# Slots and distances of the weight blocks, two steps of head 0 and the v statistics of a two-layer hybrid kernel

## The chip, the cores and the metric

One core of one Trainium2 chip runs the whole program. Its engines work beside each other, each on its own list of instructions: TensorE multiplies (PE in the profile, PEld for its weight loads), VectorE (DVE) and ScalarE (ACT) work elementwise, SyncE (SP) and GpSimd (POOL) issue transfers here. They wait for each other by semaphores. The metric is device time in microseconds (us), the median of several runs.

## The reference

Two layers over 512 latent tokens of 1024 features and 256 context tokens: layer 0 mixes the tokens by bidirectional retention with 4 heads, layer 1 by a gated unit with a spatial product (gMLP). All arithmetic is in float32.

```
for i in range(DEPTH):                       # DEPTH = 2
    shift, scale, gate = split(silu(c) @ ada_w[i] + ada_b[i])
    hx = rmsnorm(x, norm_g[i]) * (1 + scale) + shift      # hc alike, from the context
    if i == 0:   out = retention_mixer(hx, hc, ...)        # q, k, v, z = hx @ w_in; scores * decay; @ w_out
    else:        out = gmlp_chunk_mixer(hx, ...)
    x = x + gate * out
return rmsnorm(x, final_g)

def gmlp_chunk_mixer(h, w_in, vnorm_g, w_s, b_s, w_out):
    u, v, z = h @ w_in[:, :W], h @ w_in[:, W:2*W], h @ w_in[:, 2*W:]
    v = v - mean(v);  v = v * rsqrt(mean(v * v) + eps) * vnorm_g
    mixed = einsum('gij,bnjgc->bnigc', w_s, v in chunks of 128) + b_s
    return (u * mixed * silu(z)) @ w_out
```

## The kernel before

**How a product is made.** TensorE multiplies float32 in a short form, so each operand is split in two: ScalarE casts it to that form (the high half, a CAST), VectorE subtracts the high half from the operand (the low half, a TENSOR_TENSOR), and `mm3` sums three products: low x high, high x low, high x high. Weight matrices are cut in 2 x 2 blocks, and of each such product only seven are taken instead of eight (names B11, B21, T1, T2, B22, T3, T4). The T products need a difference of two weight blocks first; VectorE takes it in place, the first raw block minus the second (`raw<-raw`). The operand on the other side is a sum or difference too (the tiles `oA..`, `oS1` to `oS4`, and `rows` for the 256 context tokens).

**How weights come.** A `Stream` Q holds the order of all products and their loads. A load takes the first free slot of its list (`W` in line 215: w0 to w6, at times g0), SyncE transfers the raw block there, `upto` makes the difference and the split two products ahead of the one that TensorE is at, and `drop` frees the slot. The halves go to one of four rooms of 2112 columns with the tag hl; `split_tile` (line 97) puts them at an offset that `FORMS` (line 88) names for each kind of product: kq, v, z for layer 0's projections, wo for its output, v1 for layer 1's v, u for its u and z blocks, o for its output. All tiles stand in the order of the list in lines 91 to 95, so the list sets the addresses: slot w4 stands ahead of the 8 columns of gate0, the other w slots behind them. `t2` tiles, eleven of 512 columns, serve for what is short-lived, such as a score (pf) and its halves (ph, pl).

**What sets the order.** Every engine works off its list in the order of the text (class Queue, which records each operation, so that all of them show as line 55; transfers show as line 129). Where something is not due at once, it stands in a generator, and `aside` takes one step of it at a chosen product.

**The stages the text below speaks of:**
- V01 is the v projection of heads 0 and 1. Beside it `sums` lets VectorE and ScalarE make the operands: `sum_s2`, `sum_s4`, `sum_s3` work on the blocks of the normed input (f11, f12, f21, f22, each 1024 columns of a tile xq, in slots s0 to s3), `rows_s1` to `rows_s4` on the context (cq). `rows_s2` (line 798) writes `rows` into slot s1, f12's.
- Z23 is the z projection of heads 2 and 3, the last one. In its turns (lines 1026 to 1029) steps of `load_qk(0)` and `load_v(0)` load head 0's q, k, kc (context keys) and v, and split them (`halves`, a CAST on ScalarE and a subtraction on VectorE).
- `attend(h)` (line 1035) makes six scores of a head (`score`, 24 or 12 matmuls with qk), multiplies each by the decay table, splits it, and two steps later multiplies it by v (`pv`). Between them it takes steps of what is left of qk, v and of the output weights. A finished half is normed and gated (`gt`) and transposed (`flip`).
- V1 is layer 1's v, in two pairs p = 0, 1, each with seven turns of two halves (c). A finished block is written out, and its statistics (`bn_stats`, two of 256 columns) are put on a list, `measured`; lines 1311 and 1312 empty the list down to 4 in the first six turns of the first pair, and wholly after every later run. Lines 1324 to 1329 then merge them (`bn_aggr`), and make 1/sigma (rv, ScalarE and VectorE) and -mean/sigma (nb, line 1432).
- UZ, the last loop, is eight blocks of u and z features. `norm_vt(i)` norms a block of v (tile vt, ScalarE), and after product B22 TensorE multiplies it by the spatial weights (wsT).

Of the kernel before, what the change touches and what calls it, by code (L numbers as in the profile page):

```python
# [10 lines left out]
AF = mybir.ActivationFunctionType  # L11
ALU = mybir.AluOpType
# [56 lines left out]
def hybrid_kernel(ctx, tc, xT_d, cT_d, cv_d, sv_d, rows_d, ada0_d, adag_d, w_d, rope_d, dec_d, ws_d, id_d, out_d):  # L69
# [15 lines left out]

    T2 = 11
    HL = 4
    FORMS = {"kq": 8, "u": 8, "wo": 8, "v": 24, "z": 24, "v1": 24, "o": 32}


    for tag, size, bufs in (("hl", 2112, HL), ("t2", 512, T2), ("cv", 16, 1),
                            *((f"o{k}", 2048, 1) for k in ("A11", "A12", "A22", "S1", "S2", "S3", "S4")), ("hc", 4096, 1),
                            *((k, 1024, 1) for k in ("g2", "g3", "s0", "s2", "s3", "w4")), ("gate0", 8, 1),
                            *((k, 1024, 1) for k in ("s1", "rope", "w5", "w6", "w0", "w1", "w2", "w3", "w7", "g1", "g0")), ("dec", TW, 1)):
        st([P, size], tag, bufs=bufs, name="room")
# [116 lines left out]
            return self.tiles.pop(self.at)  # L212

    Q = Stream()
    W = [f"w{i}" for i in range(7)]
    Q.free += W + ["g0"]

    def narrow_parts(a, b, kh):
# [210 lines left out]
            load(xq[t, g], xT_d[:, 4 * g:4 * g + 4, t * HS:t * HS + HS])  # L429

    ada_w = {}
    ADA_AT = ("oS1", "oS2", "oS4", "oA22", "oS1", "oS2", "oS4", ("w7", "g1"))

    def ada0_load(kb):
        at = ADA_AT[kb]
# [357 lines left out]
    def rows_s1():  # L793
        dve.tensor_tensor(c22, c21, c22, ALU.add)
        dve.tensor_tensor(shc, sh0[:, 0:4, 1], sh0[:, 4:8, 1], ALU.add)
        rows_shifted("S1", "w7", shc)

    def rows_s2():
        dve.tensor_tensor(c22, c22, c11, ALU.subtract)
        rows_shifted("S2", "s1", sh0[:, 4:8, 1])  # L800

    def rows_s4():
        dve.tensor_tensor(c12, c12, c22, ALU.subtract)
# [194 lines left out]
    for q, name in TURNS:  # L998
        if q not in prods:
            prods[q] = project(q)  # L1000
            if q == Z23:
                Q.free.append("g0")
                qk0, v0 = load_qk(0), load_v(0)
        for c, unit in enumerate(units(q)):
            i = turn[q] = turn.get(q, -1) + 1
            if q[0] == "kq":
                prods[q].run(name, Q.get())
            else:
                prods[q].run(name, c, Q.get())
            if q == V01:  # L1010
                for made in sums.get((name, c), ()):
                    made()
                if c and name not in ("B11", "T1"):
                    popped()
                continue
            if i % 2:
                popped()
            if 1 not in pieces and (i % 2 if q == Z01 else q == V23 or i == 0):
                pieces.append(step())
            if q == V23 and i in (6, 8, 10, 12):  # L1020
                if i == 6:
                    dec0 = decay(0, ("g0", "s2"))
                aside(dec0)
            if q == Z23:
                if i in (0, 1, 2, 5, 7, 9):
                    aside(qk0)
                if i in (2, 4, 6, 11, 12):
                    aside(v0)
        if (q, name) == (V01, "T4"):
            Q.free.remove("g0")  # L1030
# [6 lines left out]
    def attend(h, qs, vs):  # L1037
        q, k, kc = qk.pop(h)
        v, z = vv.pop(h)
        dt = dts[h]  # L1040
        og = [st([P, 2, 4, HS], tag, F32R, name="og") for tag in ("oS3", "oS4")]
        steps = [(hf, j) for hf in range(2) for j in range(0, NK, 2)]
        ph, po, pend, rest = {}, {}, [], []

        def key(j):
            return (k[j // 2], j % 2) if j < NT else (kc, j - NT)

        def score(hf, j):

            p = pt(tag="tm")  # L1050
            for o in range(2):
                src, jj = key(j + 1 - o)
                for m in range(2):
                    l = (src[:, 0, m, jj * P:jj * P + P], src[:, 1, m, jj * P:jj * P + P])
                    mm3(p[:, o * HS:o * HS + HS], l, (q[hf][:, 0, m, :], q[hf][:, 1, m, :]), m == 0, m == 1)
            j1 = j + 1
            s0 = hf * HS - P * j1 + P * (NT - 1) if j < NT else XW + hf * HS - P * (j1 - NT) + P * (NC_T - 1)
            base = dt[:, s0:s0 + HS]
            both = bass.AP(base.tensor, base.offset, [base.ap[0], (P, 2), (1, HS)])
            two = lambda x: x.rearrange("p (o t) -> p o t", o=2)  # L1060
            a = t2("pf")
            dve.scalar_tensor_tensor(two(a), two(p), 1.0 / 16.0, both, ALU.mult, ALU.mult)
            hl = t2("ph", dt=F32R), t2("pl", dt=F32R)
            lows = []
            split(hl, a, lows)
            gated()
            lows[0]()
            if (hf, j) == steps[-1]:
                act.fence()
                dve.fence()  # L1070
            ph[hf, j] = hl

        def pv(hf, j):
            if j == 0:
                po[hf] = [pt(), pt()]
            h, l = ph.pop((hf, j))
            src = v[j // 2]
            for jj in range(2):
                for t in range(2):
                    o = (1 - jj) * HS + t * P  # L1080
                    mm3(po[hf][t], (h[:, o:o + P], l[:, o:o + P]), (src[:, 0, jj, :], src[:, 1, jj, :]),
                        j + jj == 0, j + jj == NK - 1)
            if j == NK - 2:
                finish(hf)

        def table():
            act.activation(root, eps, AF.Sqrt)
            yield

        def finish(hf):  # L1090
            ss = st([P, 2], "ss", bufs=2)
            for t in range(2):
                act.activation(t2("junk"), po[hf][t], AF.Square, accum_out=ss[:, t:t + 1])
            act.activation(ss, ss, AF.Sqrt, bias=eps, scale=1.0 / 512)
            rest.append((hf, ss))

        def gated():
            while rest:
                hf, ss = rest.pop(0)
                dve.reciprocal(ss, ss)  # L1100
                gts = []
                for t in range(2):
                    g = t2("gt")
                    dve.scalar_tensor_tensor(g, po[hf][t], ss[:, t:t + 1], z[:, 2 * hf + t, :], ALU.mult, ALU.mult)
                    gts.append(g)
                pend.append((hf, gts))

        def flip():
            hf, gts = pend.pop(0)
            for fp in range(2):  # L1110
                pq = pt()
                for b in range(2):
                    for t in range(2):
                        o = b * HS + t * P
                        pe.transpose(pq[:, o:o + P], gts[t][:, (2 * fp + b) * P:(2 * fp + b) * P + P], ident)
                src = pq.rearrange("p (b t) -> p b t", b=2)
                split((og[hf][:, 0, 2 * fp:2 * fp + 2, :], og[hf][:, 1, 2 * fp:2 * fp + 2, :]), src)

        LAG = 2
        wo = load_wo(h)  # L1120
        for i in range(len(steps) + LAG):
            if i < len(steps):
                score(*steps[i])
            if i >= LAG:
                pv(*steps[i - LAG])
            if i == 2:
                aside(table())
            aside(qs)
            if i > 4 or h == 0 and i < 2:
                aside(vs)  # L1130
            if i == len(steps):
                flip()
            if (h, i) == (0, 2):
                for c in range(4):
                    load(acc[:, 2 * c:2 * c + 2, :], xT_d[:, 2 * c:2 * c + 2, :])
            if i < 5:
                aside(wo)
            if i in (3, 5, 6) or (h and i == 7):
                step()
        gated()  # L1140
        return og, flip
# [166 lines left out]
    for p, name in TURNS1:  # L1308
        for c in range(2):
            pairs[p].run(name, c, Q.get())  # L1310
            while len(measured) > (4 if (p, name) in [(0, n) for n in PAIRED[:-1]] else 0):
                measured.pop(0)()
            if p == 0 and (c == 0 and name in ("B11", "B21", "T1", "T2", "B22") or (name, c) == ("B11", 1)):
                next(rest1)
# [5 lines left out]
    load(wsT, ws_d)  # L1320
    fg = st([P, D], "g0", name="fg")
    load(fg, rows_d[1:2, :].partition_broadcast(P))

    mv = st([P, NT, 2], "mv")
    for t in range(NT):
        dve.bn_aggr(mv[:, t, :], bns[:, t, :, :])
    rv = st([P, NT], "rv")
    act.activation(rv, mv[:, :, 1], AF.Sqrt, bias=eps, scale=1.0)
    dve.reciprocal(rv, rv)

    o1 = [st([P, D], f"s{t}", name="o1") for t in range(NT)]
    ya = st([P, 4, 2, SEQ], "hc", F32R, name="ya")
# [92 lines left out]
    def load_vt(i):  # L1425
        vts[i] = []
        for th in range(2):
            v = t2("vt", (P, 2, HS))
            load(v, vt_d[i // 4][i % 2][:, i // 2 % 2, 2 * th:2 * th + 2, :])
            vts[i].append(v)  # L1430

    nb = st([P, NT], "nb")
    dve.scalar_tensor_tensor(nb, mv[:, :, 0], -1.0, rv, ALU.mult, ALU.mult)

    def norm_vt(i):
        for n in range(NT):
# [26 lines left out]
        split((y[:, 0, :], y[:, 1, :]), a)  # L1463

    load_vt(0)
    norm_vt(0)
    for i in range(UZ):
        got, pms = {}, {}
        prod = Product(features, got.__setitem__)
        for name in SINGLE:  # L1470
            w = Q.get()
            settle()
            prod.run(name, w)
            if i < UZ - 1:
                if name == "T1":
                    load_vt(i + 1)
# [124 lines left out]
```

## Time and profile before

| | us |
|---|---|
| median of 3 runs | 889.34 (889.31 to 889.42) |
| the profiled execution | 890.13 |
| its span | 888.4 |

TensorE's granted clock was 0.999 of full speed over the span. The page gives each engine's busy time and its share, the chain of work that ended last, and groups of instructions; the trace adds a timeline with start, length, engine, line and operation, tiles as out<-in, and in brackets the idle time of that engine just before, with what ended it. The two largest groups of TensorE's helpers are these:

```profile
L55 DVE TENSOR_TENSOR hl<-raw,hl 128x1024 fp32r<-128x1024 f32 x195 | 236.2, 1221 | 67.3 <-ACT hl L55 66.5
L55 ACT CAST hl<-raw 128x1024 fp32r<-128x1024 f32 x195 | 203.7, 1050 | 160.2 <-PE pst L55 63.5
```

A row reads: operation, tiles and shape, count, then busy us in all and mean ns of one, then the engine's idle time just before them. VectorE made 195 low halves at 1221 ns, ScalarE as many high ones at 1050 ns.

### The profile page before, as it was taken

The page shows a single profiled execution, that of the slowest core. Times are in us where ns is not written, and L with a number is a line of the kernel's source. Part 1 is how long each engine was busy: PE and PEld are TensorE (multiplying, and loading weights), DVE is VectorE, ACT ScalarE, POOL GpSimd, SP SyncE. Part 2 cuts the span into 40 slices and gives each one's busy share as a digit, 9 for nine tenths or more (in the row PEclk, how much of TensorE's full clock was granted, in tenths as well). Part 3 has the DMA queues.
Part 4 walks back from the last instruction along what each step waited for, and adds up shares of the span by engine and source line. Part 5 has one row for each costly group of instructions (what it writes and reads, how often), then busy time and mean ns, then how long its engine had stood idle before and what let it go on. Part 6 is the DMA issues. An engine that isn't in the chain of part 4 may idle for free.

```text
span 888.4 us, 14615 instructions
## 1 busy us (share of the span) xinstructions
PE 873.1 (98%) x5670; PEld 778.8 (88%) x5670; DVE 722.8 (81%) x1016; ACT 463.1 (52%) x727; POOL 55.8 (6%) x92
## 2 busy tenths in 40 slices
PE   8999999999999999999999999999999999999997
PEld 7888898898889888999989898878999899899895
DVE  2689979988796977878687869999898578778986
ACT  5465444544524566536462559563765455255244
POOL 0001110110121020000000011102000000000000
PEclk9999999999999999999999999999999999999999
DMA  9931761972794586758175721546345045045202
GB/s 334 390 124 52 251 218 56 300 248 87 241 350 145 196 290 198 263 162 299 47 253 177 243 73 72 164 144 213 127 135 168 24 144 167 23 143 198 88 25 94
DMA packets 77092, 153.78 MB, mean 173 GB/s; under 512 B 8032, under 2 KB 35040, under 8 KB 77024
## 3 DMA queue, kind: packets, MB, share of 16 engines
q1 hardware_dynamic: 69888, 130.63, 44.9%
q0 software_dynamic: 6848, 22.03, 6.6%
q8 instruction: 44, 0.72, 0.4%
q10 hardware_dynamic: 288, 0.20, 0.1%
q14 instruction: 24, 0.20, 0.1%
HBM read 128.71 MB, written 24.12 MB: 172 GB/s over the span
## 4 chain that ended last, share of the span: by engine, by line
PE 88%; DVE 6%; ACT 3%; DMA 2%; issue 1%; SPq 0%; ACTq 0%; DVEq 0%
PE pst L55 88%; DVE hl L55 2%; DMA xq<-in_xT_dram 2%; DVE o L55 1%; DVE raw L55 1%; ACT hl L55 1%; DMA xs<-x 1%; DVE bns L55 1%; ACT f L55 0%; ACT oA L55 0%; ACT junk L55 0%; DVE ya L55 0%; DVE xq L55 0%; SPq L129 0%; ACT o L55 0%
## 5 line engine op out<-in xcount | busy, mean ns | idle before, releaser
L55 DVE TENSOR_TENSOR hl<-raw,hl 128x1024 fp32r<-128x1024 f32 x195 | 236.2, 1221 | 67.3 <-ACT hl L55 66.5
L55 ACT CAST hl<-raw 128x1024 fp32r<-128x1024 f32 x195 | 203.7, 1050 | 160.2 <-PE pst L55 63.5
L55 PE MATMUL pst<-hl,oS 128*128 128x512 f32 x576 | 137.9, 395 | 0.0
L55 PE MATMUL pst<-oS,hl 128*128 128x256 f32 x1104 | 134.7, 280 | 2.4 <-DVE hl L55 1.8
L55 PEld LDWEIGHTS pst<-oS,hl 128*128 128x128 f32 x1104 | 131.2, 188 | 3.6 <-DVE hl L55 2.2
L55 PEld LDWEIGHTS pst<-hl,oS 128*128 128x128 f32 x576 | 107.7, 187 | 27.0 <-DVE oS L55 0.4
L55 PE MATMUL pst<-oA,hl 128*128 128x256 f32 x936 | 118.2, 281 | 0.2
L55 PEld LDWEIGHTS pst<-oA,hl 128*128 128x128 f32 x936 | 112.8, 188 | 2.4 <-issue 0.8
L55 DVE TENSOR_TENSOR raw<-raw 128x1024 f32<-128x1024 f32 x92 | 111.3, 1219 | 0.8
L55 PE MATMUL pst<-hl,oA 128*128 128x512 f32 x408 | 98.6, 395 | 1.4 <-DVE hl L55 1.4
L55 PEld LDWEIGHTS pst<-hl,oA 128*128 128x128 f32 x408 | 76.0, 187 | 19.9 <-DVE hl L55 1.9
L55 PE MATMUL pst<-og,hl 128*128 128x256 f32 x768 | 92.8, 280 | 0.0
L55 PEld LDWEIGHTS pst<-og,hl 128*128 128x128 f32 x768 | 90.9, 188 | 0.8 <-issue 0.4
L55 ACT COPY snap<-pst 128x512 f32<-128x512 f32 x88 | 51.5, 587 | 70.1 <-PE pst L55 69.9
L55 PE MATMUL pst<-hl,ya 128*128 128x512 f32 (+1 forms) x300 | 69.4, 384 | 0.0
L55 PEld LDWEIGHTS pst<-hl,ya 128*128 128x128 f32 x300 | 54.7, 188 | 11.5
L55 PE MATMUL pst<-v,ph 128*128 128x512 f32 x192 | 59.7, 392 | 0.0
L55 DVE TENSOR_TENSOR snap<-pst,snap 128x512 f32<-128x512 f32 x75 | 51.2, 687 | 9.6 <-PE pst L55 9.0
L55 PEld LDWEIGHTS pst<-v,ph 128*128 128x128 f32 x192 | 36.1, 188 | 7.5
L55 ACT CAST ph<-pf 128x512 fp32r<-128x512 f32 x24 | 14.9, 622 | 51.0 <-DVE pf L55 48.3
L55 PE MATMUL pst<-v,pl 128*128 128x512 f32 x96 | 38.2, 398 | 0.0
L55 PEld LDWEIGHTS pst<-qk 128*128 128x128 f32 x288 | 35.8, 188 | 2.7 <-issue 1.6
(186 smaller groups left out, 990.6 us busy)
## 6 DMA issues: line engine op xcount, KB each, us to landing
raw<-in_w_dram SPq DMA_DIRECT2D x224, 256.0 KB, 4.3
bg<-in_adag_dram SPq DMA_DIRECT2D x32, 512.0 KB, 5.1
ada_w<-in_ada_dram SPq DMA_DIRECT2D x16, 512.0 KB, 8.9
raw<-in_w_dram SPq DMA_DIRECT2D x16, 512.0 KB, 3.9
bg<-in_dec_dram SPq DMA_DIRECT2D x12, 512.0 KB, 5.1
v<-snap POOLq DMA_DIRECT2D x16, 256.0 KB, 4.7
z<-snap POOLq DMA_DIRECT2D x16, 256.0 KB, 5.4
v<-v SPq DMA_DIRECT2D x8, 512.0 KB, 5.0
```

Of the source, the lines that this page charges most:

```text
L55: made = op(*args, **kw)
```

## The change

It has five parts:

1. `FORMS` puts the halves of v, z, v1 and o at 16 columns instead of 24 and 32, and the tile cv moves ahead of the t2 tiles, which so stand 16 columns further. In the list of weight slots w7 takes the place of w4; what used w7 (the last ada weights, rows S1) uses w4. With this, each weight block, each difference and each score stands at a multiple of 256 bytes from the operand it is worked with.
2. `rows_s2` writes into s2, f21's slot, instead of s1, f12's.
3. Head 0's decay pieces use g0 and s1 instead of g0 and s2.
4. In Z23's turn 12 two more steps of `load_qk(0)` and one more of `load_v(0)` are taken, and in head 0's attend one step of v less (its qk steps then run on into head 1's).
5. The statistics of v1 are taken at most one block a run, down to 4 in the first pair and 2 in the second; the rest, and bn_aggr, rv, nb and the first `norm_vt`, follow in the first UZ block, behind product T2.

```diff
-    FORMS = {"kq": 8, "u": 8, "wo": 8, "v": 24, "z": 24, "v1": 24, "o": 32}
-    for tag, size, bufs in (("hl", 2112, HL), ("t2", 512, T2), ("cv", 16, 1),
+    FORMS = {"kq": 8, "u": 8, "wo": 8, "v": 16, "z": 16, "v1": 16, "o": 16}
+    for tag, size, bufs in (("hl", 2112, HL), ("cv", 16, 1), ("t2", 512, T2),
...
-    W = [f"w{i}" for i in range(7)]
+    W = ["w0", "w1", "w2", "w3", "w7", "w5", "w6"]
...
-    ADA_AT = ("oS1", "oS2", "oS4", "oA22", "oS1", "oS2", "oS4", ("w7", "g1"))
+    ADA_AT = ("oS1", "oS2", "oS4", "oA22", "oS1", "oS2", "oS4", ("w4", "g1"))
...
-        rows_shifted("S1", "w7", shc)
+        rows_shifted("S1", "w4", shc)
...
-        rows_shifted("S2", "s1", sh0[:, 4:8, 1])
+        rows_shifted("S2", "s2", sh0[:, 4:8, 1])
...
-                    dec0 = decay(0, ("g0", "s2"))
+                    dec0 = decay(0, ("g0", "s1"))
...
-                if i in (0, 1, 2, 5, 7, 9):
+                for _ in range({0: 1, 1: 1, 2: 1, 5: 1, 7: 1, 9: 1, 12: 2}.get(i, 0)):
                     aside(qk0)
-                if i in (2, 4, 6, 11, 12):
+                for _ in range({2: 1, 4: 1, 6: 1, 11: 1, 12: 2}.get(i, 0)):
                     aside(v0)
...
-            if i > 4 or h == 0 and i < 2:
+            if i > 4 or h == 0 and i < 1:
                 aside(vs)
...
-            while len(measured) > (4 if (p, name) in [(0, n) for n in PAIRED[:-1]] else 0):
+            if len(measured) > (4 if p == 0 else 2):
                 measured.pop(0)()
...
-    mv = st([P, NT, 2], "mv")
-    for t in range(NT):
-        dve.bn_aggr(mv[:, t, :], bns[:, t, :, :])
-    rv = st([P, NT], "rv")
-    act.activation(rv, mv[:, :, 1], AF.Sqrt, bias=eps, scale=1.0)
-    dve.reciprocal(rv, rv)
...
+    rv = st([P, NT], "rv")
     nb = st([P, NT], "nb")
-    dve.scalar_tensor_tensor(nb, mv[:, :, 0], -1.0, rv, ALU.mult, ALU.mult)
+
+    def spread_v():
+        mv = st([P, NT, 2], "mv")
+        for t in range(NT):
+            dve.bn_aggr(mv[:, t, :], bns[:, t, :, :])
+        act.activation(rv, mv[:, :, 1], AF.Sqrt, bias=eps, scale=1.0)
+        dve.reciprocal(rv, rv)
+        dve.scalar_tensor_tensor(nb, mv[:, :, 0], -1.0, rv, ALU.mult, ALU.mult)
...
     load_vt(0)
-    norm_vt(0)
...
             prod.run(name, w)
+            if measured:
+                measured.pop(0)()
+            if i == 0 and name == "T2":
+                while measured:
+                    measured.pop(0)()
+                spread_v()
+                norm_vt(0)
```

Three places of VectorE's order. In V01, from the low half of operand S4 (oS_1027) on, `rows<-cq,sh_152` being rows S2 and `xq<-xq` the difference f11 - f21; - is before, + after:

```order
 L55 TENSOR_TENSOR oS_1027<-xq,oS_1027 128x1024
 L55 TENSOR_TENSOR raw<-raw 128x1024
+L55 TENSOR_TENSOR xq<-xq 128x1024
+L55 TENSOR_TENSOR cq<-cq 128x4x128
+L55 TENSOR_TENSOR hl<-raw,hl 128x1024
 L55 SCALAR_TENSOR_TENSOR rows<-cq,sh_152,rows 128x128 x4
-L55 TENSOR_TENSOR xq<-xq 128x1024
-L55 TENSOR_TENSOR hl<-raw,hl 128x1024 x2
+L55 TENSOR_TENSOR hl<-raw,hl 128x1024
```

The four rows moved behind the difference of xq, the one of cq and one low half.

In V1, at the end of the first pair, where TensorE waits at 583.09 before; the half it waits for is the first of the three in the last row (of before):

```order
L55 BN_STATS bns<-snap 128x6 x3
L55 TENSOR_TENSOR hl<-raw,hl 128x1024
L55 BN_STATS bns<-snap 128x6 x8
L55 TENSOR_TENSOR raw<-raw 128x1024 x3
L55 TENSOR_TENSOR hl<-raw,hl 128x1024 x3
```

The same place after the change:

```order
L55 BN_STATS bns<-snap 128x6
L55 TENSOR_TENSOR hl<-raw,hl 128x1024
L55 BN_STATS bns<-snap 128x6 x2
L55 TENSOR_TENSOR raw<-raw 128x1024
L55 BN_STATS bns<-snap 128x6 x2
L55 TENSOR_TENSOR raw<-raw 128x1024
L55 TENSOR_TENSOR hl<-raw,hl 128x1024
L55 TENSOR_TENSOR raw<-raw 128x1024
L55 TENSOR_TENSOR hl<-raw,hl 128x1024
```

Between the half in the second row and the one TensorE waits for stood eight statistics and three differences; now four statistics and two differences stand there, and the others follow one by one.

In the first UZ block, from the last statistics of V1 on, of before (`mv` is bn_aggr's result; the difference of T1 is the first raw row, that of T2 the third):

```order
L55 BN_STATS bns<-snap 128x6 x4
L55 TENSOR_TENSOR hl<-raw,hl 128x1024
L55 BN_AGGR mv<-bns 128x2
L55 TENSOR_TENSOR raw<-raw 128x1024
L55 BN_AGGR mv<-bns 128x2
L55 BN_STATS bns<-snap 128x6 x2
L55 TENSOR_TENSOR raw<-raw 128x1024
L55 TENSOR_TENSOR hl<-raw,hl 128x1024
L55 BN_STATS bns<-snap 128x6 x2
L55 BN_AGGR mv<-bns 128x2 x2
L55 TENSOR_TENSOR raw<-raw 128x1024
L55 RECIPROCAL rv<-rv 128x4
```

And after the change:

```order
L55 TENSOR_TENSOR hl<-raw,hl 128x1024
L55 BN_STATS bns<-snap 128x6
L55 TENSOR_TENSOR raw<-raw 128x1024
L55 BN_STATS bns<-snap 128x6 x3
L55 TENSOR_TENSOR raw<-raw 128x1024
L55 TENSOR_TENSOR hl<-raw,hl 128x1024
L55 BN_STATS bns<-snap 128x6
L55 TENSOR_TENSOR raw<-raw 128x1024
L55 BN_STATS bns<-snap 128x6 x3
L55 BN_AGGR mv<-bns 128x2 x2
L55 TENSOR_TENSOR hl<-raw,hl 128x1024
L55 BN_AGGR mv<-bns 128x2 x2
```

The last low half of the second piece is T2's, which before follows behind the first piece's end. Between T1's half (the second low half in each) and T2's difference now stands one statistic, not two and two aggregates; three statistics and two aggregates lie between that difference and its half, and 1/sigma (rv) follows later.

## The prediction

> **What bounds the kernel now.** I read the profiled page first (busy time, then the chain that ended last), then TensorE's waits after the start-up, then the timeline of the engines around each of them.
>
> ```profile
> span 888.4 us, 14615 instructions
> PE 873.1 (98%) x5670; PEld 778.8 (88%) x5670; DVE 722.8 (81%) x1016; ACT 463.1 (52%) x727; POOL 55.8 (6%) x92
> DVE  2689979988796977878687869999898578778986
> PE 88%; DVE 6%; ACT 3%; DMA 2%; issue 1%; SPq 0%; ACTq 0%; DVEq 0%
> PE pst L55 <- DVE hl L55: 3.2, 3, 1.4
> PE pst L55 <- issue: 1.4, 1, 1.4
> ```
>
> TensorE works 873.1 of 888.4 us; the row of digits is VectorE's busy share in 40 slices, in tenths. The last two lines are its waits from 57 us on: three for a low half (hl) that VectorE makes, 3.2 us together, and one of 1.4 us. Whatever the change does to VectorE, ScalarE and the queues, only TensorE's waits can give time; the change leaves its own instructions and their order alone. Three waits are worth the name:
>
> ```profile
> 337.58 1.64 PE L55 MATMUL pst<-qk 128*128 128x256 f32 x12 [1.41 <-issue]
> 583.09 2.13 PE L55 MATMUL pst<-hl,oA 128*128 128x512 f32 x8 [1.41 <-DVE hl L55]
> 626.49 3.09 PE L55 MATMUL pst<-oS,hl 128*128 128x256 f32 x24 [1.36 <-DVE hl L55]
> ```
>
> The columns are start, length, engine, work, and in brackets the idle time before it. The first is the third score of head 0 in attend, the second the second half of turn T4 of the first v1 pair, the third product T2 of the first feature block (i = 0 in the last loop). 1.41 + 1.41 + 1.36 = 4.18 us is all that these places can give.
>
> **The change part by part.** *Respacing (FORMS, the room list, w7 for w4).* Before, the 195 low-half subtractions don't stand at one distance: their rooms start 8, 24 or 32 columns in, and w4 lies ahead of the 8 columns of gate0, other slots behind. Yet their durations (minimum, median, maximum) are one number:
>
> ```profile
> L55 DVE TENSOR_TENSOR hl<-raw,hl x195: 1207/1222/1229, 14.1 to 866.7; 128x1024 fp32r<-128x1024 f32 x195
> L55 DVE TENSOR_TENSOR raw<-raw 128x1024 f32<-128x1024 f32 x92 | 111.3, 1219 | 0.8
> ```
>
> A distance that mattered would split this group. Its ends bound the price: from 15 ns less than the median to 7 ns more for one subtraction, and the 92 differences of weights (1219 ns) look the same. I take zero: VectorE is idle for 165.6 us (888.4 - 722.8), and a few ns hide there. The Trainium skill ("SBUF — State Buffer", section on the two separate sides) speaks against this part: by it engines are held up in SBUF by the port pair that VectorE and GpSimd share and by no bandwidth limit, so a distance between operands has no place to act. By that rule the sum below stays as it is; the narrow row agrees.
>
> *Two qk halves and a v half of head 0 in Z23 instead of attend.* The first wait:
>
> ```profile
> 330.13 1.23 DVE L55 TENSOR_TENSOR v<-v 128x1024 fp32r<-128x1024 f32 x1 [1.64 <-ACT v L55]
> 334.81 0.69 DVE L55 SCALAR_TENSOR_TENSOR pf<-pst,dt 128x512 f32<-128x512 f32 x1 [3.45 <-PE pst L55]
> 336.80 0.69 DVE L55 TENSOR_TENSOR qk<-qk 128x512 fp32r<-128x512 f32 x1
> 353.56 1.14 ACT L55 CAST qk<-qk 128x512 fp32r<-128x512 f32 x2
> 630.11 2.00 ACT L55 CAST hl<-raw 128x1024 fp32r<-128x1024 f32 x2
> 343.23 0.39 PE L55 MATMUL pst<-v,pl 128*128 128x512 f32 x1
> 354.37 0.74 DVE L55 SCALAR_TENSOR_TENSOR gt<-pst,ss,z 128x512 f32<-128x512 f32 x1
> 357.09 1.04 PE L55 MATMUL pst<-ident,gt 128*128 128x128 f32 x8
> 329.07 1.03 ACT L55 CAST v<-v 128x1024 fp32r<-128x1024 f32 x1
> 332.01 0.60 ACT L55 ACTIVATE snap<-pst 128x512 f32<-128x512 f32 x1 [1.91 <-PE pst L55]
> ```
>
> The third score needs the context keys' low half, which ends at 336.80 + 0.69 = 337.49; TensorE goes on 0.09 us later. VectorE sat idle for 3.45 us before 334.81. After the change ScalarE casts qk, qk, v, v from 329.07 (two more at 0.53 and one at 0.95 us a step, the pairs of casts in the fence less one length: to 332.1, as the z eviction of 332.01 falls due, which is then about 0.05 us late), and VectorE subtracts to 333.5, still ahead of 334.81. The score follows the second one with no gap: **-1.41 us**. What is late next is the second score's low part (pl), about 339.2 by the same steps, against a need at 343.23 - 1.41 = 341.8: 2.6 us to spare. Where the halves of head 1 move two steps up, VectorE has 1.2 us more ahead of the second gt; some of it fills idle time, and gt ends about 0.8 later than its 355.1, needed at 357.09 (both in the clock of before, less 1.41 after).
>
> *Statistics of v1 one pair a run.* The second wait:
>
> ```profile
> 574.68 1.21 DVE L55 TENSOR_TENSOR hl<-raw,hl 128x1024 fp32r<-128x1024 f32 x1
> 575.80 2.70 DVE L55 BATCH_NORM_STATS2 bns<-snap 128x6 f32<-128x256 f32 x8
> 578.42 3.48 DVE L55 TENSOR_TENSOR raw<-raw 128x1024 f32<-128x1024 f32 x3
> 581.82 3.49 DVE L55 TENSOR_TENSOR hl<-raw,hl 128x1024 fp32r<-128x1024 f32 x3
> ```
>
> Eight statistics (2.70 us, 0.33 a step) and three differences (1.13 a step) stand ahead of the half that TensorE waits for, which ends at 583.04. After: the half, two statistics, a difference, two statistics, a difference, then that half. The half at 574.68 starts two statistics earlier and ends its step at 574.68 - 0.66 + 1.13 = 575.15: 575.15 + 0.66 + 1.13 + 0.66 + 1.13 = 578.73, ScalarE's cast of the first difference is done by 578.8, and the half ends at 580.0. TensorE wants it at 583.09 - 1.41 = 581.68: **-1.41 us**, 1.6 to spare.
>
> *The rest of them and the spread (bn_aggr, rv, nb) behind UZ0's T2.* The third wait:
>
> ```profile
> 614.57 1.40 DVE L55 BATCH_NORM_STATS2 bns<-snap 128x6 f32<-128x256 f32 x4
> 622.37 0.59 DVE L55 BATCH_NORM_AGGREGATE mv<-bns 128x2 f32<-128x48 f32 x2
> 622.88 1.16 DVE L55 TENSOR_TENSOR raw<-raw 128x1024 f32<-128x1024 f32 x1
> 625.21 1.23 DVE L55 TENSOR_TENSOR hl<-raw,hl 128x1024 fp32r<-128x1024 f32 x1 [0.89 <-ACT hl L55]
> 624.13 1.05 ACT L55 CAST hl<-raw 128x1024 fp32r<-128x1024 f32 x1 [0.83 <-DVE rv L55]
> 637.92 1.95 PE L55 MATMUL pst<-wsT,vt 128*128 128x128 f32 x16
> ```
>
> Before, T2's difference (622.88) stands behind two statistics and two aggregates, and cast and half follow it one after the other. After, one statistic stands between T1's half and it, and the rest lies beside the cast. From 614.57 with the same steps: a half 615.70, one statistic 616.03, T1's difference 617.16, three statistics 618.15, a difference 619.28, T1's half 620.41 (needed at 622), one statistic 620.74, T2's difference 621.87 (cast on ScalarE by 623.0), three statistics and two aggregates 623.46, and T2's half ends at 624.68. TensorE wants it at 626.49 - 1.36 = 625.13: **-1.36 us**, with only 0.45 to spare. The spread then gives nb at about 629 and the four vt at 631, still ahead of the matmul that reads them (637.92 before, about 636.5 then).
>
> *Rows S2 in s2.* Slot s2 is xq's block f21, and VectorE must have taken f11 - f21 (the xq row) before it can be overwritten; before, s1 was long free.
>
> ```profile
> 83.96 1.22 DVE L55 TENSOR_TENSOR raw<-raw 128x1024 f32<-128x1024 f32 x1
> 85.10 1.14 DVE L55 SCALAR_TENSOR_TENSOR rows<-cq,sh,rows 128x128 fp32r<-128x128 f32 x4
> 86.15 1.22 DVE L55 TENSOR_TENSOR xq<-xq 128x1024 f32<-128x1024 f32 x1
> L55 DVE SCALAR_TENSOR_TENSOR rows<-cq,sh,rows x4: 348/349/351, 85.1 to 85.9; 128x128 fp32r<-128x128 f32 x4
> L55 ACT ACTIVATE rows<-cq,sh x4: 393/393/406, 84.4 to 85.3; 128x128 fp32r<-128x128 f32 x4
> 84.39 1.28 ACT L55 ACTIVATE rows<-cq,sh 128x128 fp32r<-128x128 f32 x4
> 85.57 1.05 ACT L55 CAST hl<-raw 128x1024 fp32r<-128x1024 f32 x1
> 87.64 1.32 PEld L55 LDWEIGHTS pst<-hl,rows 128*128 128x128 f32 x6
> ```
>
> Queued behind the xq subtraction on VectorE now stand cq, one low half, and then the rows: 85.10 + 1.13 + 0.61 + 1.13 = 87.97. On ScalarE two casts (0.95 a step, the first behind a copy, from 85.75) stand ahead of the four rows, which so begin at 87.7; a row of 128 takes 0.39 there and 0.35 on VectorE. First low row: about 88.1 + 0.35 = 88.48, against the weight load at 87.64: a **new wait, +0.85 us**. Bounds: 0.4, if the copy and the casts come off 0.4 earlier and the low half of VectorE with them, and 1.3, about the size of the three waits now there. I take 0.85, the walk's own number. Behind the rows wait the S3 operand and the next halves; they come later by no more than TensorE itself then is, so no second wait follows.
>
> *The rest.* Head 0's decay pieces, the slot of the last ada weights and some loads on SP's queue change places.
>
> ```profile
> raw<-in_w_dram SPq DMA_DIRECT2D x224, 256.0 KB, 4.3
> ```
>
> A weight block lands 4.3 us after its issue, and the loads that change places are issued a product (2.96 us of TensorE) or several ahead of their use. I take 0; at worst one comes late by a part of that, 0.4.
>
> **Sum.** -1.41 - 1.41 - 1.36 + 0.85 = -3.33 us. The profiled execution took 890.13 us (888.4 of span, 1.7 around it), 0.79 over the median of the runs shown. 890.13 - 3.33 = 886.80 there; on the median of 889.34 it is **886.0 us**.
>
> **The rivals.** *Two of the three go, one stays* (the third, with its margin of 0.45 us, or its like in a neighbouring product as the statistics now lie there): -3.33 + 1.36 = -1.97, so 887.4 us. For it speaks that the margin is one statistic and a bit; against it, that every step is the pitch of a row. *The waits are replaced*: TensorE catches up 4.2 us on an engine that is 81% busy, and the next half behind each place is late instead; at half of the sum of 4.18 plus 1.3 at the rows, 889.34 - 2.09 + 1.3 = 888.5 us, within the noise. Against it: slack of 1.6 and 2.6 us behind the first two. It is also the case in which the change doesn't do what it says. *Operands at a distance of 0 collide* (the slower side): a two-input operation would take longer in the stretches where the slices show VectorE 9 tenths busy or more, twelve of 22.2 us with some 18 such operations each. Up to a tenth of a slice, 2.2 us or 122 ns each, would hide. To end 1.8 us slower it must eat 3.3 + 1.8 = 5.1 us, 0.43 a slice, so (2.2 + 0.43) / 18 = 146 ns for each; from there on it decides, and at 200 ns it costs 12 x (18 x 0.2 - 2.2) = 16.8 us: 889.3 - 3.3 + 16.8 = 902.8 us. The longest of 195 is 7 ns over the median with distances mixed, and that is against it. The mirror of it, that the distance saves, falls by the same row.
>
> **How the numbers follow.** Forecast (all three go, rows wait 0.4 to 1.3): 0.62, at 885.5 to 886.5. One stays: 0.18, 887.4, straddling the bound of no change. Replaced: 0.13. Collision or another loss: 0.04; the rows wait hidden after all, 885.2: 0.03. A measurement of this kernel can tell 0.2%, 1.78 us, from no change: faster is under 887.56, which takes the forecast, the 885.2 case and two thirds of the second: 0.77. Same has the rest of it and the third case, 0.19; slower 0.04. The range reaches from the hidden rows wait (885.2, less 0.2 for what the respacing may give) to the end of the second case with 1.3 at the rows (887.4 + 0.45) and a short wait of 0.4: 885.0 to 888.2.
>
> **What would show it.** In the profile after: TensorE without idle time near 336, 581 and 624 us; one new wait of about 0.85 us near 87.6, released by VectorE's rows; the group of 195 halves still at 1.22 us. Wrong are the steps if a wait of more than 0.4 stands at any of the three places, if the rows are on time, if TensorE's total idle time after 57 us isn't about 3.3 us less, or if the group's mean moves by over 15 ns.

## The result, and the profile after

The changed kernel takes 877.04 us (876.50 to 877.42, 4 runs) against 889.33 before (889.11 to 889.42, 4 runs): a ratio of 0.9862, 95% interval 0.9845 to 0.9879. The forecast was 886.0, and its range reached down to 885.0 only. The profiled execution took 877.42 us, 12.7 less than that of before.

The page of the changed kernel, and under it TensorE's waits from 57 us on:

```profile
span 875.6 us, 14616 instructions
PE 862.4 (98%) x5670; PEld 777.2 (89%) x5670; DVE 721.8 (82%) x1016; ACT 461.1 (53%) x727; POOL 55.8 (6%) x92
L55 DVE TENSOR_TENSOR hl<-raw,hl 128x1024 fp32r<-128x1024 f32 x195 | 236.7, 1222 | 61.2 <-ACT hl L55 59.6
PE pst L55 <- DVE rows L55: 0.7, 1, 0.7
PE pst L55 <- DVE hl L55: 0.6, 1, 0.6
```

Two things changed on TensorE. Its waits fell from 5.0 us (3.2 + 1.4 before, and two of 0.2 that stayed) to 1.7 (0.7 + 0.6 and the same two): 3.3 us, what the prediction had added up. And its own busy time fell from 873.1 to 862.4 us with the same 5670 matmuls. That nobody had forecast. VectorE's 195 low halves stayed at 1222 ns.

The waits, place by place, in TensorE's timeline after (start, length, work, count; idle time before it in brackets):

```profile
329.45 4.36 PE L55 MATMUL pst<-qk 128*128 128x256 f32 x36
566.23 11.04 PE L55 MATMUL pst<-hl,oA 128*128 128x512 f32 x48
612.56 5.76 PE L55 MATMUL pst<-oS,hl 128*128 128x256 f32 x48
88.36 1.66 PE L55 MATMUL pst<-hl,rows 128*128 128x512 f32 x6 [0.72 <-DVE rows L55]
831.19 3.09 PE L55 MATMUL pst<-oS,hl 128*128 128x256 f32 x24 [0.57 <-DVE hl L55]
```

The first three scores (36 matmuls), turn T4 of v1's first pair (48), and products T1 and T2 of the first feature block (48) each run through: the three waits of before are gone. Instead there is the wait at rows S2, 0.72 us. The last row is a wait in a late feature block, 0.39 us before at 843.81.

The busy time, in the groups of TensorE's instructions with their shapes (count, then busy us, mean ns of one), before:

```profile
L55 PE MATMUL pst<-hl,oS 128*128 128x512 f32 x576 | 137.9, 395 | 0.0
L55 PE MATMUL pst<-hl,oA 128*128 128x512 f32 x408 | 98.6, 395 | 1.4 <-DVE hl L55 1.4
L55 PE MATMUL pst<-hl,ya 128*128 128x512 f32 x276 | 66.6, 394 | 0.0
L55 PE MATMUL pst<-hl,rows 128*128 128x512 f32 x96 | 24.7, 392 | 0.0
L55 PE MATMUL pst<-oA,hl 128*128 128x256 f32 x936 | 118.2, 281 | 0.2
```

and after:

```profile
L55 PE MATMUL pst<-hl,oS 128*128 128x512 f32 x576 | 134.2, 390 | 0.1
L55 PE MATMUL pst<-hl,oA 128*128 128x512 f32 x408 | 95.8, 390 | 0.0
L55 PE MATMUL pst<-hl,ya 128*128 128x512 f32 x276 | 65.6, 389 | 0.0
L55 PE MATMUL pst<-hl,rows 128*128 128x512 f32 x96 | 24.5, 391 | 0.7 <-DVE rows L55 0.7
L55 PE MATMUL pst<-oA,hl 128*128 128x256 f32 x936 | 117.9, 281 | 0.2
```

The mean of every group of 512 columns whose operands the change moved is shorter by 1 to 6 ns; one group of 24, hl_e,oA, whose operands stand at the same distance in both kernels, has 394 ns in both. The large groups of 256 columns stay within 1 ns. Matmuls overlap, so what counts is the step from the start of one to the start of the next. The longest blocks without a wait, in Z23, before and after:

```profile
299.61 22.56 PE L55 MATMUL pst<-hl,oS 128*128 128x512 f32 x96
322.01 11.36 PE L55 MATMUL pst<-hl,oA 128*128 128x512 f32 x48
```

```profile
296.81 21.92 PE L55 MATMUL pst<-hl,oS 128*128 128x512 f32 x96
318.57 11.04 PE L55 MATMUL pst<-hl,oA 128*128 128x512 f32 x48
```

96 matmuls took 322.01 - 299.61 = 22.40 us, 233.3 ns each; after, 318.57 - 296.81 = 21.76 us, **226.7 ns** each. What differs between them is where the two operands of the matmul stand. Each matmul has a standing operand, which a LDWEIGHTS row of 128x128 (PEld, 188 ns in the mean) loads first, and a moving one of 512 or 256 columns. By the addresses of the built programs, the moving operand (the weights' halves in an hl room, 512 columns) was 32 bytes off the standing one (oS, oA, hc, half of rows) modulo 256 before, and 64 bytes off in the output products (ya, yb) and in score x v; after, 0 in all of them. All distances below are counted like this, address of the moving operand less that of the standing one, modulo 256 bytes. The tile list gives the same: a room is 33 times 256 bytes, cv is 64 bytes, so oS stands at 64; the halves stood at 24 x 4 = 96 before and stand at 16 x 4 = 64 after.

So where part 1 says "the operand it is worked with", that is TensorE's other operand in the 512-column matmuls. It doesn't hold for all weight blocks: the 256-column matmuls of kq, u and wo, where hl stands still, are 32 bytes off in both kernels, and on VectorE nearly all low halves now stand 32 or 64 bytes from their raw blocks.

### The profile page after: what moved, and what is told of

Read it like the earlier page. It is cut to its first block, busy times and chain, and to the rows that moved or that the text cites. A ratio compares the mean times of both kernels' runs of the same rounds, so it can differ in the third digit from the quotient of the medians.

```text
span 875.6 us, 14616 instructions
## 1 busy us (share of the span) xinstructions
PE 862.4 (98%) x5670; PEld 777.2 (89%) x5670; DVE 721.8 (82%) x1016; ACT 461.1 (53%) x727; POOL 55.8 (6%) x92
## 4 chain that ended last, share of the span: by engine, by line
PE 86%; DVE 8%; ACT 3%; issue 1%; DMA 1%; SPq 1%; DVEq 0%; ACTq 0%
PE pst L55 86%; DVE hl L55 2%; DVE o L55 2%; DMA xq<-in_xT_dram 1%; DVE raw L55 1%; ACT hl L55 1%; DVE xq L55 1%; DVE ya L55 1%; SPq L129 1%; ACT f L55 1%; DVE oS L55 0%; ACT oA L55 0%; ACT junk L55 0%; DVE cq L55 0%; DVE snap L55 0%
## 5 line engine op out<-in xcount | busy, mean ns | idle before, releaser
L55 DVE TENSOR_TENSOR hl<-raw,hl 128x1024 fp32r<-128x1024 f32 x195 | 236.7, 1222 | 61.2 <-ACT hl L55 59.6
L55 PE MATMUL pst<-hl,oS 128*128 128x512 f32 x576 | 134.2, 390 | 0.1
L55 PE MATMUL pst<-oA,hl 128*128 128x256 f32 x936 | 117.9, 281 | 0.2
L55 PE MATMUL pst<-hl,oA 128*128 128x512 f32 x408 | 95.8, 390 | 0.0
L55 DVE SCALAR_TENSOR_TENSOR acc<-pst,gate,acc 128x256 f32<-128x256 f32 x64 | 29.1, 480 | 12.1 <-PE pst L55 12.0
```

The costliest lines, as they stand in the source:

```text
L55: made = op(*args, **kw)
```

## The experiments

The runs of one batch share those of the kernel before: 889.95 us in the first batch (e1 to e4), one run of 890.16 in the second (e5 to e7), 890.03 in the last (e8, e3b, e9).

**e1: the spacing alone.** The kernel before with

```diff
-    FORMS = {"kq": 8, "u": 8, "wo": 8, "v": 24, "z": 24, "v1": 24, "o": 32}
-    for tag, size, bufs in (("hl", 2112, HL), ("t2", 512, T2), ("cv", 16, 1),
+    FORMS = {"kq": 8, "u": 8, "wo": 8, "v": 16, "z": 16, "v1": 16, "o": 16}
+    for tag, size, bufs in (("hl", 2112, HL), ("cv", 16, 1), ("t2", 512, T2),
...
-    W = [f"w{i}" for i in range(7)]
+    W = ["w0", "w1", "w2", "w3", "w7", "w5", "w6"]
...
-        rows_shifted("S1", "w7", shc)
+        rows_shifted("S1", "w4", shc)
```

(and w4 for w7 in ADA_AT).

> The kernel before with part 1 of the change alone: FORMS, cv ahead of t2, w7 for w4, rows S1 in w4 (rows S2 stays in s1, so 24 weight loads of it stay 32 bytes off). Theory A: a 512-column matmul is issued every 227 ns if its two operands stand at a multiple of 256 bytes, every 234 ns at 32 and about 231 at 64 bytes, whatever VectorE does; all 512-column groups of TensorE then fall to a mean of about 389 to 391 ns, TensorE's busy time by about 9 us, its three waits (1.41, 1.41, 1.36) stay, and the time is about 880 us (879 to 881.5). Rival B: the time comes from VectorE's and ScalarE's operands (their steps get shorter, TensorE waits less): low halves under 1215 ns, waits gone. Rival C: the time comes from the moved work, and the spacing does nothing: 889.3 us.

Measured: 881.24 us, ratio 0.9902 (0.9886 to 0.9918). Its page, its waits, and two of its waits in the timeline:

```profile
PE 863.3 (98%) x5670; PEld 777.4 (88%) x5670; DVE 721.6 (82%) x1016; ACT 462.5 (53%) x727; POOL 56.0 (6%) x92
PE pst L55 <- DVE hl L55: 3.6, 3, 1.7
PE pst L55 <- issue: 1.4, 1, 1.4
332.31 1.64 PE L55 MATMUL pst<-qk 128*128 128x256 f32 x12 [1.41 <-issue]
576.60 2.79 PE L55 MATMUL pst<-hl,oA 128*128 128x512 f32 x11 [1.66 <-DVE hl L55]
```

TensorE's busy time falls by 9.8 us with the old order of work and all the old waits. The second is longer, 1.66 us for 1.41: TensorE got there 6.7 us earlier than before (574.94 for 581.68), the low half only 6.5 (576.60 for 583.09). Theory A holds; B and C fall.

**e2: the moved work alone.** The changed kernel with FORMS, the tile list, slots, rows S2 and the decay pieces of before.

```diff
-    FORMS = {"kq": 8, "u": 8, "wo": 8, "v": 16, "z": 16, "v1": 16, "o": 16}
+    FORMS = {"kq": 8, "u": 8, "wo": 8, "v": 24, "z": 24, "v1": 24, "o": 32}
...
-        rows_shifted("S2", "s2", sh0[:, 4:8, 1])
+        rows_shifted("S2", "s1", sh0[:, 4:8, 1])
```

> The changed kernel with parts 1 to 3 undone (old FORMS, old slots, rows S2 in s1, decay pieces as before): only the two qk halves and the v half in Z23 and the spread statistics are left. Theory A: the three waits of 4.18 us go and nothing else, 885.2 us (884.8 to 885.8), TensorE's busy time stays at 873 us. Rival C: about 877 us, all of the gain.

Measured: 885.25 us, ratio 0.995 (0.9934 to 0.9966), TensorE as it was, and one wait for a low half left, the late one of 0.4:

```profile
PE 872.7 (99%) x5670; PEld 778.8 (88%) x5670; DVE 723.3 (82%) x1016; ACT 461.3 (52%) x727; POOL 55.8 (6%) x92
PE pst L55 <- DVE hl L55: 0.4, 1, 0.4
```

The moves are worth about the three waits: 889.95 - 885.25 = 4.7 us in this batch (3.0 to 5.9 by the interval), 4.1 against the 889.33 of the result, for 4.18 us of waits.

**e3 and e3b: rows S2 back in s1.** The changed kernel with

```diff
-        rows_shifted("S2", "s2", sh0[:, 4:8, 1])
+        rows_shifted("S2", "s1", sh0[:, 4:8, 1])
...
-                    dec0 = decay(0, ("g0", "s1"))
+                    dec0 = decay(0, ("g0", "s2"))
```

> The changed kernel with rows S2 back in s1 and head 0's decay pieces back in g0 and s2. Theory A: TensorE's wait of 0.7 us at rows S2 goes, 24 matmuls of rows S2 go back to a step of 234 ns instead of 227 (0.17 us): 0.5 us less than the changed kernel, 876.5 us. Rival: that wait only moves to the next product, 877.0 us or more.

> e3 once more, beside e8 on the same chip: 876.0 us, 0.4 to 1.2 under the changed kernel's 877.04.

Measured: 875.98 us (875.87 to 876.21), ratio 0.9842 (0.9825 to 0.9860), and 876.08 (875.87 to 876.89), ratio 0.9846 (0.9831 to 0.9861). The wait for rows is gone from the list of waits, and none takes its place there. The medians are 1.0 us under the changed kernel, where 0.5 was expected; the intervals of the ratios overlap, so only the wait itself is shown. In the profiled executions 0.6 us of the difference lies ahead of rows S2: the 512-column matmuls begin at 60.27 us in the changed kernel and at 59.69 in e3. It is the fastest of the kernels that ran. e1 and e2 are its two halves, and they add up: 8.7 and 4.7 us under the 889.95 of their batch, 13.4 of e3's 14.0.

e3 also answers a rival that e1 leaves: that the place of the moving operand by itself matters, and not its distance from the standing one. Rows S1 stand in w4, at distance 0, rows S2 in s1, at 224 (32 the other way), and both meet halves at the same 16 columns. The second half of rows S1, the first of rows S2, and the row behind each, in e3:

```profile
82.87 1.52 PE L55 MATMUL pst<-hl,rows 128*128 128x512 f32 x6
84.23 2.89 PE L55 MATMUL pst<-hl,oS 128*128 128x512 f32 x12
86.96 1.56 PE L55 MATMUL pst<-hl,rows 128*128 128x512 f32 x6
88.36 2.89 PE L55 MATMUL pst<-hl,oS 128*128 128x512 f32 x12
```

(84.23 - 82.87) / 6 = 226.7 ns at 0, (88.36 - 86.96) / 6 = 233.3 at 224: it is the distance.

**e4: other distances at 512 columns.** e3 with

```diff
-    FORMS = {"kq": 8, "u": 8, "wo": 8, "v": 16, "z": 16, "v1": 16, "o": 16}
+    FORMS = {"kq": 8, "u": 8, "wo": 8, "v": 20, "z": 48, "v1": 0, "o": 40}
```

> The kernel of e3 with other offsets of the rooms: v at 20 columns (16 bytes off its other operand), z at 48 (128 bytes), v1 at 0 (192 bytes), o at 40 (96 bytes). All is computed as before. Theory A1, only a multiple of 256 is short: all four kinds are issued every 231 to 235 ns, 512-column groups back at 394 to 395 ns, about 885 us. Theory A2, the period is 128 or 64 bytes: z (and v1, if 64) stay at 227 ns, the others at 234, about 880 us. Rival B or C: no change against e3, 876.5 us.

Measured: 883.52 us in one run. TensorE's timeline in v (16 bytes), z (128) and v1 (192), each with the row behind it, and the group of the output products (96):

```profile
206.85 2.94 PE L55 MATMUL pst<-hl,oA 128*128 128x512 f32 x12
209.63 1.55 PE L55 MATMUL pst<-hl,hc 128*128 128x512 f32 x6
...
298.04 22.47 PE L55 MATMUL pst<-hl,oS 128*128 128x512 f32 x96
320.35 11.32 PE L55 MATMUL pst<-hl,oA 128*128 128x512 f32 x48
...
580.24 22.56 PE L55 MATMUL pst<-hl,oS 128*128 128x512 f32 x96
602.63 11.36 PE L55 MATMUL pst<-hl,oA 128*128 128x512 f32 x48
...
L55 PE MATMUL pst<-hl,ya 128*128 128x512 f32 x276 | 67.3, 395 | 0.0
```

| distance in bytes, modulo 256 | step of a 512-column matmul |
|---|---|
| 0 (e3, after) | 226.7 ns |
| 16 | 2.78 us / 12 = 231.7 |
| 32 (before) | 233.3 |
| 64 (before, output) | 233.3 in one block of 96, 229.1 where ya and yb take turns |
| 96 (ya) | (700.41 - 677.99) / 96 = 233.5 |
| 128 | 22.31 / 96 = 232.4 |
| 192 | 22.39 / 96 = 233.2 |
| 224 (e3, rows S2) | 233.3 |

The two values at 64 are (707.88 - 685.48) / 96 and (772.85 - 750.86) / 96 by the starts of the blocks; why they differ is open. Theory A1: of the distances tried only 0 is short; 128 isn't, so the period isn't 128 or 64.

**e5, e6, e7, e9, e8: the distance at 256 columns.** e3 with kq, u and wo moved, three distances a kernel; the first and the last of them:

```diff
-    FORMS = {"kq": 8, "u": 8, "wo": 8, "v": 16, "z": 16, "v1": 16, "o": 16}
+    FORMS = {"kq": 16, "u": 24, "wo": 0, "v": 16, "z": 16, "v1": 16, "o": 16}
...
+    FORMS = {"kq": 32, "u": 32, "wo": 32, "v": 16, "z": 16, "v1": 16, "o": 16}
```

> The kernel of e3 with other offsets for the weights that stand still in the 256-column matmuls (8 columns, 32 bytes off, in every kernel so far): kq at 16 columns (0 bytes off), u at 24 (224 bytes), wo at 0 (64 bytes). Theory N1, a multiple of 256 bytes is short at 256 columns too: the 888 matmuls of kq go from a step of 117 ns to about 113 (3 us), the others stay or get longer. Theory N2, as the 24 narrow matmuls of hl,ya show (120 ns at 0, 118 at 64 bytes): 0 is the longest here, kq +3 ns (2.7 us more), wo +1 ns (0.8 us); u unknown; 877 to 883 us in all, against 876.0 of e3.

> As e5 with kq at 12 columns (16 bytes off), u at 4 (48 bytes), wo at 10 (24 bytes). N1: all between 113 and 117 ns. N2: 117 to 120, none under the 117 ns of 32 bytes; 876 to 883 us. If one of them is under 116 ns, that distance beats the 32 bytes of all kernels so far.

> As e5 with kq at 32 columns (192 bytes off), u at 48 (128 bytes), wo at 56 (96 bytes). N1: 117 ns or more, since no multiple of 256. N2: wo near 120 ns as the narrow hl,ya at 96 bytes (e4), u and kq unknown, 117 to 121; 877 to 885 us.

> The kernel of e3 with kq, u and wo all at 32 columns, so that all 3000 256-column matmuls with hl stand 192 bytes off their other operand. By e7 a step there takes 116.0 to 116.3 ns instead of 116.8: 3000 x 0.6 ns = 1.8 us less, 874.2 us against e3's 876.0. Rival: the 0.6 ns were those of e7's stage alone (kq) and wo and u don't follow: 875 us or more.

> As e8 with kq at 28 columns (208 bytes off), u at 36 (176 bytes), wo at 40 (160 bytes): whether 192 is the low point of a slope or a point of its own. Slope: 116.5 to 118 ns at all three; single point: 118 to 120 ns beside it. 876 to 883 us.

Measured: e5 881.19, e6 877.95, e7 881.73, e9 881.23 us in one run each, e8 877.06 us (4 runs; ratio 0.9854, 0.9838 to 0.9870). A block of 48 in a kq stage of e3 (32 bytes off) and the row behind it, and the same of e5 (0 bytes):

```profile
185.92 5.76 PE L55 MATMUL pst<-oS,hl 128*128 128x256 f32 x48
191.52 2.96 PE L55 MATMUL pst<-oA,hl 128*128 128x256 f32 x24
```

```profile
187.01 5.92 PE L55 MATMUL pst<-oS,hl 128*128 128x256 f32 x48
192.77 3.04 PE L55 MATMUL pst<-oA,hl 128*128 128x256 f32 x24
```

(191.52 - 185.92) / 48 = 116.7 ns, and (192.77 - 187.01) / 48 = **120.0 ns** at 0. By the same reading, kq and u give (at 128 bytes the blocks of e7's u stage differ):

| bytes off | 0 | 16 | 32 | 48 | 128 | 176 | 192 | 208 | 224 |
|---|---|---|---|---|---|---|---|---|---|
| step, ns | 120.0 | 117.3 | 116.7 | 116.7 | 118.5 to 120.0 | 118.5 | 117.9 or 113.3 | 118.3 | 118.3 |

The first block of wo gives 118.3 at 24 bytes, 117.7 at 64, 120.0 at 96 and 117.5 at 160. N2 holds: what is best for 512 columns is the worst, with 96 and part of 128, for 256. The 32 bytes that the kernel before and the changed one have there are among the best. At 192 two stages of one kernel (e7) with the same offsets differ:

```profile
186.13 5.82 PE L55 MATMUL pst<-oS,hl 128*128 128x256 f32 x48
191.79 2.99 PE L55 MATMUL pst<-oA,hl 128*128 128x256 f32 x24
...
281.59 5.60 PE L55 MATMUL pst<-oS,hl 128*128 128x256 f32 x48
287.03 2.88 PE L55 MATMUL pst<-oA,hl 128*128 128x256 f32 x24
```

117.9 ns in the first, 113.3 in the second. I had read their mean, 116.1, as the price of that distance, and so e8's expectation failed: its u blocks take 117.7 to 117.9 ns; 113.3 comes again in that kq stage, in a block of 24 of the first kq stage ((56.67 - 53.95) / 24) and in 34 matmuls of wo (113.5, from 422.83 to 426.69), which is too little, and e8 came out 1.0 us over e3b in place of 1.8 under it.

## Why the prediction was wrong

**The respacing, taken at zero.** This is the step that failed. It took the operands in question for those of VectorE's subtractions, whose row (1207 to 1229 ns) excluded an effect there. That was right: the group is at 1222 ns after, too. But the respacing also moves TensorE's operands against each other, and I bounded nothing for the engine that is busy 98% of the time. "The change leaves its own instructions and their order alone" was true, and yet the step from one to the next fell from 233.3 to 226.7 ns. The size: 1104 matmuls that were 32 bytes off (576 + 408 + 72 of hc + 48 of rows) x 6.6 ns = 7.3 us, and by their groups 1.8 us for those at 64 bytes (ya 1.0, yb 0.2, v with the score halves 0.6), 9.1 in all; e1, where 24 matmuls of rows S2 lose their distance of 0 (0.16 us), is 8.7 us under the kernel before with 0.4 more of waits after 57 us, so 9.1 where 8.9 are due. The page shows 9.8 less busy time there; the other 0.7 is spread over groups that differ by a few tenths and isn't explained.

The trace of before held a hint that the prediction doesn't use: rows with a mean of 392 ns beside oS and oA with 395. Half of the rows matmuls stood at distance 0 already. A few ns look like noise, but 3 ns times the 1764 matmuls of 512 columns that stood elsewhere are 5 us.

The rule of the Trainium skill that I weighed there ("SBUF — State Buffer", on the two separate sides: engines with ports of their own never wait on each other) is about engine against engine; the reading that a distance between operands then has no place to act is contradicted by 226.7 and 233.3 ns at two distances of one engine's operands. The Trainium skill's figure for an isolated 512-column matmul ("TensorE: Matmul & The Clock Gate", section "Back-to-back issue gap": 518 cycles, about 216 ns) lies under both.

**The three waits: right.** 1.41, 1.41 and 1.36 us are gone after, and in e2, with the moves alone, too; its time fell by 4.7 us in its batch, 4.1 against the 889.33 of the result, for 4.18. The third was called with 0.45 us to spare; after, its half starts at 613.94, ends 1.17 later at 615.11, and the block of 48 goes on without a gap, T2's matmuls starting at about 612.56 + 24 x 0.1167 = 615.36: 0.25 to spare.

```profile
613.44 0.59 DVE L55 BATCH_NORM_AGGREGATE mv<-bns 128x2 f32<-128x48 f32 x2
613.94 1.17 DVE L55 TENSOR_TENSOR hl<-raw,hl 128x1024 fp32r<-128x1024 f32 x1
```

The margin is 0.2 smaller than walked; a TensorE that gets there faster, which the walk had left out, is the likely cause.

**Rows S2: right.** 0.85 us was forecast, 0.72 came, by the chain that was named. After, on VectorE:

```profile
85.08 1.23 DVE L55 TENSOR_TENSOR xq<-xq 128x1024 f32<-128x1024 f32 x1
86.21 0.70 DVE L55 TENSOR_TENSOR cq<-cq 128x512 f32<-128x512 f32 x1
86.81 1.23 DVE L55 TENSOR_TENSOR hl<-raw,hl 128x1024 fp32r<-128x1024 f32 x1
87.95 1.14 DVE L55 SCALAR_TENSOR_TENSOR rows<-cq,sh,rows 128x128 fp32r<-128x128 f32 x4
```

The walk had the rows behind 87.97 and waiting for ScalarE till 88.1; ScalarE was ready. e3 shows what the slot bought: 0.72 us of wait were paid for 24 matmuls x 6 ns = 0.14 us.

**The rest at zero:** in the first 57 us the waits rose from 3.3 to 4.6 us (those for transfers from 1.4 to 3.1), of which 0.3 is left at 60 us by the starts of the matmuls; the late wait grew by 0.2. **The sum** of -3.33 us is thus what e2 and the wait at rows give; the forecast lacked 9 us of another kind. **The rivals:** a stall that stays, and replaced waits, did not come; "operands at a distance of 0 collide" named the right quantity on the wrong engine and with the wrong sign; its "mirror", dismissed with it by the same row, is what happened, on TensorE.

## What to carry to other kernels

Where an engine is busy 98% of the time, a change of addresses is priced first on that engine's own operands: divide a block without a wait by its count, and compare blocks whose operands stand differently before calling a few ns noise. Then fix the spacing for each shape by itself, since 512 and 256 columns want different distances here. A slot chosen for spacing can cost a wait that is larger than the spacing's gain, as rows S2 did.

## What the runs showed of the hardware

- A float32 matmul of 512 columns (in the short form, with a new weight load each) is issued every 226.7 ns with its two operands at a multiple of 256 bytes from each other (0, 256, 512 and 768 modulo 1024 all occur in these blocks), and every 231.7 to 233.5 ns at 16, 32, 96, 128, 192 and 224 bytes (e3, e4 and before); at 64 bytes 229.1 and 233.3 were seen. The reason (who reads what at the same time, the weights of this matmul or those of the next) wasn't tried.
- With 256 columns the step is 116.7 ns at 32 and 48 bytes (e3, e6), 120.0 at 0 (e5) and 118.5 to 120.0 at 128 (e7).
- At 192 bytes the same matmuls run at 117.9 ns in one stage and at 113.3 in another (e7, e8), block after block. It looks like two states of one stream, but what picks between them stays open.
